# A two-layer encoder step on one core: low parts of the paired weights on VectorE, later transposes of v, and separate PSUM banks for the heads' outputs

## The chip, the cores and the metric

The kernel is one program on one core of a Trainium2 chip. The time is the device time of an execution in microseconds (us); the number compared is the median of the runs. TensorE (PE) does the matrix products, VectorE (DVE) and ScalarE (ACT) the element-wise work and the copies out of PSUM, GpSimd (POOL) a little element-wise work and the issue of some DMAs, and SyncE (SP) issues most DMAs.

## What is computed

One inference step of an encoder with two layers over 512 prompt frames and 64 frames of a running stream, 576 columns in all, with a model width of 2048. Layer 0 is gated linear attention, layer 1 a convolution module. Cut to what matters here, layer 0 is:

```python
proj = h @ w_in                       # h: rmsnorm of x; w_in: 2048 x 6160
q, k, v, r, a1 = jnp.split(proj, ...) # 1024, 1024, 2048, 2048, 16 columns
loga = jax.nn.log_sigmoid(a1 @ w_a2 + b_a) / GATE_NORM
# per head (4 heads, dk 256, dv 512), in chunks, with a decaying state S:
b = jnp.cumsum(ac, axis=-2)
att = jnp.where(mask, einsum('td,sd->ts', qc * exp(b), kc * exp(-b)), 0.0)
o = att @ vc + (qc * exp(b)) @ S
S = exp(b_last)[:, None] * S + (kc * exp(b_last - b)).T @ vc
y = (rmsnorm(o) * silu(r)) @ w_out
```

Layer 1 and the final norm follow; the change does not touch them. All tensors are float32.

## The kernel before

**Precision.** A float32 product is made of three TensorE products in a faster float format: a weight is split into a high part (whi, a rounded copy on ACT) and a low part (wlo, raw minus whi), the activations likewise (names that end in h and l), and hi x hi, hi x lo and lo x hi are added. A unit is a pair (whi, wlo) of 128 x 8 x 128 elements; each of the two has four buffers, used in turn. `to_unit` makes a unit. Its low part is made in one of two ways: by a subtraction on DVE (L126), or, when `src` is given, by a negated copy on ACT (L128) to which a DMA issued by POOL adds the weights from DRAM once more (L129).

**The pair stage** (126 to 498 us of the profile). Fourteen pairs of 128-column weight blocks (eight pairs of v, the two of head 1's q and k, four of r) are each computed by `run_full` in a Strassen-like scheme: seven products of 24 matmuls in place of eight (`step(0)` to `step(6)`, with sums S1 to S4 of activation blocks and differences of weight blocks on DVE, L184). The four raw weight blocks of a pair are r1 (two buffers, ra and rb), r2 and r4 (two buffers shared), and r3 (one buffer). A step makes sure that the units up to four steps ahead have been asked for (`ensure`, LEAD = 4). The results are collected in PSUM tiles d11, d12, d21 (a pool of four banks) and db, and copied to two SBUF tiles ta and tb (`t1`, `t2`) of a tag s2 with six buffers. `done` then handles each of the two. For q, k and r it writes the tile to DRAM. For v (`v_done`) it transposes the tile on TensorE into token order (`to_tok`: four transposes into ptv, one into puv, in PSUM tiles of the tag ms), splits it on ACT and DVE and writes four pieces to the DRAM tensor vd with SP's queue.

**The heads** (498 to 792 us). For each of four heads: the decay (`decay`: small matmuls pz at L778, then exponentials, logarithms and scans on ACT and DVE), the scores (`attention`: pa at L844 and L854, transposes of the keys), the outputs (`output`: po at L889 for the prompt, pq at L894 and L897 for the stream, copied by ACT at L891 and by DVE at L898), the states (`states`: pS at L920) and the norm (m_o at L458). The remaining projections (`tile`, 24 products of 48 matmuls, tiles ps) are interleaved by the scheduler with the head's own work. The PSUM tiles pz, pa, pt, pu, po, pq, pS and m_o all share the two banks of the tag ms. The projections take two banks each from `main_tile`: two of three times from the pool of four banks, every third time from the two banks of the tag main.

**What sets the order.** The program is written in the order of the Python code; a list scheduler then orders each engine's instructions by priority and readiness at build time. Weight splitting has a raised priority. On the chip each engine runs its list in that order and waits on semaphores.

Of the kernel before, what the change touches and what calls it, by code (L numbers as in the profile page):

```python
# [11 lines left out]
F32 = mybir.dt.float32  # L12
# [5 lines left out]
P = 128  # L18
# [31 lines left out]
def emit(nc, tc, x, wg, wa1, wa2, wgo, wc, wco, par, s0, y, sp_out, ss_out, cv_out):  # L50
# [30 lines left out]
    def psum_pool(key, name, bufs):  # L81
        psum[key] = tc.tile_pool(name=name, bufs=bufs, space=PSUM)
        return psum[key].__enter__()
# [6 lines left out]
    px = psum_pool("e", "pse", 1)  # L90
    pool_s = [px]
# [12 lines left out]
    def tmp(name, w=T, dt=F32):  # L104
        return s2.tile([P, w], dt, tag="s2", name=name)
# [8 lines left out]
    def load_raw(src, half, name, p=None, tag="raw"):  # L114
        raw = (p or wraw).tile([P, 8, P], F32, tag=tag, name=name)
        state["dma"] = nc.sync.dma_start(raw, src[:, half * 8 : half * 8 + 8, :])
        return raw

    def to_unit(i, raw, w=8, src=None):

        hi = whl.tile([P, 8, P], F32R, tag="whi", name=f"whi{i}")
        lo = whl.tile([P, 8, P], F32R, tag="wlo", name=f"wlo{i}")
        with tc.high_priority(offset=PRIO):
            nc.scalar.activation(hi[:, :w, :], raw, AF.Copy)  # L124
            if src is None:
                nc.vector.tensor_tensor(lo[:, :w, :], raw, hi[:, :w, :].bitcast(F32), ALU.subtract)  # L126
            else:
                nc.scalar.activation(lo, raw, AF.Copy, scale=-1.0)  # L128
                nc.gpsimd.dma_start(lo, src, accum_op=ALU.add)  # L129
        ready[i] = (hi, lo)  # L130
# [46 lines left out]
    def plan_full(w1, w2, ra):  # L177


        d = {}  # L180

        def diff(out, a, b):
            with tc.high_priority(offset=PRIO):
                nc.vector.tensor_tensor(out, a, b, ALU.subtract)  # L184

        def u0(i):
            d["r1"] = load_raw(w1, 0, f"raw{i}", sp, ra)
            to_unit(i, d["r1"], src=w1[:, :8, :])

        def u1(i):  # L190
            d["r2"] = load_raw(w2, 0, f"raw{i}")
            diff(d["r1"], d["r2"], d["r1"])
            to_unit(i, d["r1"])

        def u2(i):
            d["r3"] = load_raw(w2, 1, f"raw{i}", sp, "r3")
            diff(d["r2"], d["r3"], d["r2"])
            diff(d["r1"], d["r3"], d["r1"])
            to_unit(i, d["r1"])

        def u4(i):
            d["r4"] = load_raw(w1, 1, f"raw{i}")
            to_unit(i, d["r4"], src=w1[:, 8:, :])

        def u5(i):
            diff(d["r1"], d["r4"], d["r1"])
            to_unit(i, d["r1"])

        chunks.extend([u0, u1, u2, lambda i: to_unit(i, d["r2"]), u4, u5,
                       lambda i: to_unit(i, d["r3"], src=w2[:, 8:, :])])  # L210

    def ensure(n):
        while state["n"] < min(n, len(chunks), state["cap"]):
            i = state["n"]
            state["n"] += 1
            chunks[i](i)
# [27 lines left out]
    rot = {"n": 0}  # L244

    def bank(name):
        return psb.tile([P, 512], F32, tag="bank", name=name)[:, :HT]

    def main_tile(name):

        rot["n"] += 1
        if pool_s[0] is not None and rot["n"] % 3 == 0:
            return [pool_s[0].tile([P, 512], F32, tag="main", bufs=2, name=f"{name}_{j}")[:, :HT] for j in range(2)]
        return [bank(f"{name}_{j}") for j in range(2)]

# [123 lines left out]
    def operand(n, k):  # L379
        if n in sums8:  # L380
            return [sums8[n][k // 2][:, part, k % 2, :] for part in range(2)]
        j = 0 if n in ("A11", "A12") else 1
        k += 8 if n in ("A12", "A22") else 0
        return [a[k][:, j * HT : (j + 1) * HT] for a in (ah, al)]

    def prod8(dst, n, unit, first):
        hi, lo = unit
        for k in range(8):
            a, b = operand(n, k)
            for i, (w, v) in enumerate(((hi, a), (hi, b), (lo, a))):  # L390
                nc.tensor.matmul(dst, w[:, k, :], v, start=first and k == 0 and i == 0,  # L391
                                 stop=k == 7 and i == 2, skip_group_check=True)

    def run_full(c, f1, f2, func, done, middle=None):

        c11, c12, c21 = (bank(f"d{n}_{f1}") for n in ("11", "12", "21"))
        pb = pool_s[0].tile([P, 512], F32, tag="main", bufs=2, name=f"db_{f1}")[:, :HT]
        sh = tmp(f"sh{f1}", HT)
        t1, t2 = tmp(f"ta{f1}"), tmp(f"tb{f1}")
        w = t2[:, HT:]  # L400

        def step(i, dst, n, first):
            ensure(c + i + LEAD)
            prod8(dst, n, ready.pop(c + i), first)

        add = nc.vector.tensor_tensor
        step(0, c11, "A11", True)
        nc.scalar.activation(sh, c11, AF.Copy)
        step(1, c12, "S1", True)
        if middle:  # L410
            middle()
        step(2, pb, "S2", True)
        add(sh, sh, pb, ALU.add)
        step(3, c21, "S3", True)
        add(w, sh, c21, ALU.add)
        add(w, w, c12, ALU.add)
        step(4, c11, "A12", False)
        nc.scalar.activation(t1[:, :HT], c11, func)
        step(5, c21, "A22", False)
        add(t1[:, HT:], sh, c21, ALU.add)  # L420
        if func != AF.Copy:
            nc.scalar.activation(t1[:, HT:], t1[:, HT:], func)
        done(f1, t1)
        step(6, c12, "S4", False)
        add(t2[:, :HT], sh, c12, ALU.add)
        if func != AF.Copy:
            nc.scalar.activation(t2, t2, func)
        done(f2, t2)

    def run_plain(c, f1, f2, addend, evac):  # L430

# [113 lines left out]
    def page(i, shape, name, dt=F32):  # L545

        return sp.tile(shape, dt, tag=i if isinstance(i, str) else f"pg{i}", name=name)
# [33 lines left out]
    for half, aw in enumerate(a1w):  # L581
        src = a1r[:, 8 * half : 8 * half + 8, :].unsqueeze(2).broadcast_to([P, 8, 3, RANK])
# [61 lines left out]
    w2 = page(9, [96, 1024], "w2s", F32R)  # L644
# [105 lines left out]
    for i, (b, n) in enumerate(gla_pairs):  # L750
        run_full(base_p + 7 * i, b, b + 1, AF.Silu if n == "r" else AF.Copy, v_done if n == "v" else to_dram,
                 restore if i == len(gla_pairs) - 1 else None)
    sums8.clear()
    pools.pop().__exit__(None, None, None)

# [120 lines left out]
    def output(h):  # L876
        d = hd[h]
        q, att, v = d["qs"], d["att"], d["v"]
        d["s0"] = s0t = gp.tile([P, 2, DVH], F32, tag="s0", name=f"s0_{h}")
        nc.sync.dma_start(s0t, s0[:, 2 * h : 2 * h + 2, :])  # L880
        ob = big.tile([P, 4, T], F32, tag="big", name=f"o{h}")
        sq = stat.tile([P, T], F32, tag="ssq", name=f"osq{h}")
        pairs = products(v, att)
        for vt in range(4):
            vc = slice(vt * P, vt * P + P)
            po = px.tile([P, 512], F32, tag="ms", bufs=2, name=f"po{h}{vt}")
            for i in range(4):
                for n, (a, b) in enumerate(pairs):
                    nc.tensor.matmul(po[:, i * P : TP], a[:, i, vc], b[:, OFFS[i] : OFFS[i] + TP - i * P],  # L889
                                     start=(i == 0 and n == 0), stop=(i == 3 and n == 2), skip_group_check=True)  # L890
            nc.scalar.activation(ob[:, vt, :TP], po, AF.Copy)  # L891
            po = px.tile([P, 512], F32, tag="ms", bufs=2, name=f"pq{h}{vt}")
            for dt in range(2):
                nc.tensor.matmul(po[:, :TS], s0t[:, dt, vt * P : (vt + 1) * P], q[:, dt, :],  # L894
                                 start=(dt == 0), stop=False)
            for n, (a, b) in enumerate(pairs):
                nc.tensor.matmul(po[:, :TS], a[:TS, 4, vc], b[:TS, 1280:1344], start=False, stop=(n == 2))  # L897
            nc.vector.tensor_copy(ob[:, vt, TP:T], po[:, :TS])  # L898
            add_sq(sq, ob[:, vt, :], vt == 0, f"o{h}{vt}")
        d.update(o=ob, sq=sq)  # L900
# [41 lines left out]
    def start_head(h):  # L942
        hd[h] = {}
        decay(h)
# [12 lines left out]
    def gates(h):  # L957
        for vt in range(4 if h < 3 else 1):
            rblk(h, vt)
# [10 lines left out]
    def tile(i, ins=None):  # L970
        with tc.issue_after(ins) if ins is not None else nullcontext():
            run_groups(gla_last[i : i + 1], heads_evac, base_l + 2 * i)

    start_head(0)
    scores(0)
    tile(0)
    values(0)
    for h in range(H):
# [13 lines left out]
        if h < 3:  # L992
            tile(2 * h + 3, turned)
            values(h + 1)
    gates(3)
    tile(9, turned)


# [340 lines left out]
```

## Time and profile before

| | |
|---|---|
| median of 3 runs | 1823.49 us (1821.79 to 1824.61) |
| profiled execution | 1826.77 us, span 1825.0 us |
| mean granted TensorE clock | 0.985 |
| PE busy | 1736.3 us, 95% |
| DVE, ACT, POOL busy | 59%, 52%, 29% |
| DMA, accumulating and others from POOL's queue (q0) | 99.86 MB, 27.9% of 16 engines' span |
| DMA from SP's queue (q1) | 202.33 MB, 36.8% |

A row of the stages gives the length of a stretch, then for PE, weight loads (PEld), DVE, ACT and POOL the busy time and the number of instructions in it, then the granted clock, the mean busy share of the 16 DMA engines and GB/s. A row of waits says which engine and line waited for which, the sum in us, how many times, and the longest. A row of groups ends with busy time, mean ns of one, and idle time before it with what ended it. A row of the chain or the timeline starts with the time from the start of the span and a length. Names stand without buffer numbers there.

### The profile page before, as it was taken

The page shows a single profiled execution, that of the slowest core. Times are in us where ns is not written, and L with a number is a line of the kernel's source. Part 1 is how long each engine was busy: PE and PEld are TensorE (multiplying, and loading weights), DVE is VectorE, ACT ScalarE, POOL GpSimd, SP SyncE. Part 2 cuts the span into 40 slices and gives each one's busy share as a digit, 9 for nine tenths or more (in the row PEclk, how much of TensorE's full clock was granted, in tenths as well). Part 3 has the DMA queues.
Part 4 walks back from the last instruction along what each step waited for, and adds up shares of the span by engine and source line. Part 5 has one row for each costly group of instructions (what it writes and reads, how often), then busy time and mean ns, then how long its engine had stood idle before and what let it go on. Part 6 is the DMA issues. An engine that isn't in the chain of part 4 may idle for free.

```text
span 1825.0 us, 31131 instructions
## 1 busy us (share of the span) xinstructions
PE 1736.3 (95%) x12606; PEld 1702.0 (93%) x12606; DVE 1069.2 (59%) x1580; ACT 943.9 (52%) x1271; POOL 526.1 (29%) x497
## 2 busy tenths in 40 slices
PE   9999988899898998999999999999999999999996
PEld 8998888889898887999999999999999999999995
DVE  7764453544334355195557788878888761185554
ACT  7754443435565556463236555656555574453333
POOL 3100100001121333202222455545555452223221
PEclk9999999999999999999999999999999999999998
DMA  7966857667796776544444777777777768713323
GB/s 241 242 157 165 206 134 190 173 168 181 189 271 173 211 225 185 146 165 153 144 133 140 166 165 165 165 165 166 163 166 165 178 144 185 158 54 133 110 94 129
DMA packets 114944, 304.18 MB, mean 167 GB/s; under 512 B 11344, under 2 KB 37840, under 8 KB 113776
## 3 DMA queue, kind: packets, MB, share of 16 engines
q1 hardware_dynamic: 87632, 202.33, 36.8%
q0 software_dynamic: 27168, 99.86, 27.9%
q8 instruction: 99, 1.62, 0.4%
q14 instruction: 45, 0.37, 0.1%
HBM read 264.70 MB, written 37.45 MB: 166 GB/s over the span
## 4 chain that ended last, share of the span: by engine, by line
PE 74%; DMA 10%; DVE 7%; issue 5%; ACT 3%; SPq 1%; POOL 0%; DVEq 0%; ACTq 0%; POOLq 0%
PE ps L227 15%; PE ps L230 15%; PE ps L224 15%; PE c L337 8%; PE c L328 6%; PE d L391 5%; DMA raw<-wg 4%; DMA wlo<-wg 3%; PE db L391 2%; PE pS L920 1%; PE cb L328 1%; DVE c L1174 1%; PE po L889 1%; DVE wlo L126 1%; PE pq L337 1%
## 5 line engine op out<-in xcount | busy, mean ns | idle before, releaser
L124 ACT ACTIVATE whi<-raw 128x1024 fp32r<-128x1024 f32 x296 | 312.5, 1058 | 515.9 <-PE ps L227 170.0
L227 PE MATMUL ps<-h1l,whi 128*128 128x288 f32 x1536 | 329.7, 296 | 0.0
L224 PE MATMUL ps<-h1h,whi 128*128 128x288 f32 x1536 | 329.7, 296 | 0.0
L230 PE MATMUL ps<-h1h,wlo 128*128 128x288 f32 x1536 | 329.5, 296 | 0.0
L1111 DVE SCALAR_TENSOR_TENSOR acc<-ux,pr,acc 128x606 f32<-128x606 f32 x352 | 297.7, 852 | 11.8 <-ACT acc L1101 2.2
L230 PEld LDWEIGHTS ps<-h1h,wlo 128*128 128x128 f32 x1536 | 248.3, 189 | 0.0
L227 PEld LDWEIGHTS ps<-h1l,whi 128*128 128x128 f32 x1536 | 248.3, 189 | 0.0
L224 PEld LDWEIGHTS ps<-h1h,whi 128*128 128x128 f32 x1536 | 248.2, 189 | 0.0
L126 DVE TENSOR_TENSOR wlo<-raw,whi 128x1024 fp32r<-128x1024 f32 x126 | 157.1, 1247 | 113.9 <-ACT whi L124 112.5
L129 POOL DMA_DIRECT2D wlo<-wg x78 | 67.9, 871 | 506.0 <-ACT wlo L128 350.0
L128 ACT ACTIVATE wlo<-raw 128x1024 fp32r<-128x1024 f32 x170 | 177.2, 1042 | 0.0
L1109 POOL TENSOR_TENSOR sd<-sd,sd 128x606 f32<-128x606 f32 x96 | 153.3, 1597 | 72.5 <-ACT sd L1105 71.2
L391 PE MATMUL d<-nh,wlo 128*128 128x288 f32 x448 | 135.8, 303 | 13.5 <-DMA wlo<-wg 13.5
L608 POOL TENSOR_TENSOR ssq<-ssq,sq_x 128x576 f32<-128x576 f32 x35 | 63.3, 1810 | 295.6 <-ACT sq_x L607 289.4
L129 POOL DMA_DIRECT2D wlo<-wc x92 | 80.8, 879 | 218.7 <-ACT wlo L128 165.3
L391 PE MATMUL d<-nh,whi 128*128 128x288 f32 x448 | 135.5, 303 | 0.0
L391 PE MATMUL d<-nl,whi 128*128 128x288 f32 x448 | 135.0, 301 | 0.0
L184 DVE TENSOR_TENSOR raw<-raw,raw 128x1024 f32<-128x1024 f32 x56 | 68.4, 1223 | 86.4 <-DMA raw<-wg 73.4
L1105 ACT ACTIVATE sd<-ux,pr 128x606 f32<-128x606 f32 x112 | 87.3, 793 | 55.8 <-POOL sd L1109 55.8
L227 PE MATMUL ps<-nl,whi 128*128 128x288 f32 x480 | 108.7, 303 | 0.0
L230 PE MATMUL ps<-nh,wlo 128*128 128x288 f32 x480 | 105.2, 300 | 2.8 <-DMA wlo<-wg 2.8
L224 PE MATMUL ps<-nh,whi 128*128 128x288 f32 x480 | 106.8, 304 | 0.0
(542 smaller groups left out, 3904.4 us busy)
## 6 DMA issues: line engine op xcount, KB each, us to landing
raw<-wc SPq DMA_DIRECT2D x96, 512.0 KB, 4.9
raw<-wg SPq DMA_DIRECT2D x94, 512.0 KB, 6.0
wlo<-wc POOLq DMA_DIRECT2D x92, 512.0 KB, 7.6
wlo<-wg POOLq DMA_DIRECT2D x78, 512.0 KB, 8.5
raw<-wco SPq DMA_DIRECT2D x26, 512.0 KB, 3.8
raw<-wgo SPq DMA_DIRECT2D x25, 512.0 KB, 4.3
ld<-pd SPq DMA_DIRECT2D x29, 288.0 KB, 6.9
vd<-v SPq DMA_DIRECT2D x32, 256.0 KB, 6.5
```

The source lines that it names most:

```text
L124: nc.scalar.activation(hi[:, :w, :], raw, AF.Copy)
L126: nc.vector.tensor_tensor(lo[:, :w, :], raw, hi[:, :w, :].bitcast(F32), ALU.subtract)
L128: nc.scalar.activation(lo, raw, AF.Copy, scale=-1.0)
L129: nc.gpsimd.dma_start(lo, src, accum_op=ALU.add)
L224: nc.tensor.matmul(ps[j], hi[:, kk, :], ah[k][:, j * HT : (j + 1) * HT], start=st, stop=False)
L227: nc.tensor.matmul(ps[j], hi[:, kk, :], al[k][:, j * HT : (j + 1) * HT], start=False, stop=False)
L230: nc.tensor.matmul(ps[j], lo[:, kk, :], ah[k][:, j * HT : (j + 1) * HT], start=False, stop=sp)
L328: nc.tensor.matmul(dst, w[:, o + k, :], v, start=start and k == 0 and i == 0, stop=stop and k == 3 and i == 2, skip_group_check=True)
L337: nc.tensor.matmul(dst[j], w[:, k, :], v[:, j * HT : (j + 1) * HT], start=start[j] and k == 0 and i == 0, stop=stop[j] and k == 7 and i == ...
L391: nc.tensor.matmul(dst, w[:, k, :], v, start=first and k == 0 and i == 0, stop=k == 7 and i == 2, skip_group_check=True)
L1109: nc.gpsimd.tensor_tensor(side, side, t, ALU.add)
L1111: nc.vector.scalar_tensor_tensor(a, v3(u[:, w : w + CW]), cw(w), a, ALU.mult, ALU.add)
```

## The change

Three edits:

1. In the pair stage all low parts are made on DVE: three units of each pair lose `src`.
2. The calls of `done` are kept in a list `later`, and the first two steps of the next pair each call one of them after their product; what is left runs after the last pair.
3. In the heads po takes its tiles from the tag main in place of ms, and the projections' tiles always come from the pool of four banks while the flag `heads` is set.

```diff
@@ plan_full
-            to_unit(i, d["r1"], src=w1[:, :8, :])
+            to_unit(i, d["r1"])
...
-            to_unit(i, d["r4"], src=w1[:, 8:, :])
+            to_unit(i, d["r4"])
...
-                       lambda i: to_unit(i, d["r3"], src=w2[:, 8:, :])])
+                       lambda i: to_unit(i, d["r3"])])
@@ main_tile
-        if pool_s[0] is not None and rot["n"] % 3 == 0:
+        if pool_s[0] is not None and rot["n"] % 3 == 0 and not rot.get("heads"):
@@ run_full
+    later = []
...
             prod8(dst, n, ready.pop(c + i), first)
+            if i < 2 and later:
+                later.pop(0)()
...
-        done(f1, t1)
         step(6, c12, "S4", False)
...
-        done(f2, t2)
+        later.extend([lambda: done(f1, t1), lambda: done(f2, t2)])
@@ after the loop over gla_pairs
+    while later:
+        later.pop(0)()
@@ output
-            po = px.tile([P, 512], F32, tag="ms", bufs=2, name=f"po{h}{vt}")
+            po = px.tile([P, 512], F32, tag="main", bufs=2, name=f"po{h}{vt}")
@@ before and after the heads
+    rot["heads"] = True
     start_head(0)
...
     gates(3)
+    rot.update(n=0, heads=False)
     tile(9, turned)
```

TensorE at the end of the first v pair, before: the last matmuls of the sixth product (d21), two transposes of ta, then the seventh product (d12).

```order
L391 MATMUL d21_4_1459<-nh14_1031,wlo21_1526 128x288
L391 MATMUL d21_4_1459<-nh15_1036,whi21_1525 128x288
L391 MATMUL d21_4_1459<-nl15_1037,whi21_1525 128x288
L391 MATMUL d21_4_1459<-nh15_1036,wlo21_1526 128x288
L729 MATMUL ptv4_1652<-ident_89,ta4_1462 128x128 x2
L391 MATMUL d12_4_1458<-S4_0_1050,whi22_1554 128x288 x2
```

And after: ta's transposes stand behind the first product of the second pair (d11_6) and ahead of its second (d12_6).

```order
L391 MATMUL d11_6_1678<-nh7_996,whi23_1584 128x288
L391 MATMUL d11_6_1678<-nl7_997,whi23_1584 128x288
L391 MATMUL d11_6_1678<-nh7_996,wlo23_1585 128x288
L732 MATMUL ptv4_1716<-ident_89,ta4_1461 128x128 x4
L735 MATMUL puv4_1723<-ident_89,ta4_1461 64x128
L391 MATMUL d12_6_1679<-nh0_957,whi24_1616 128x288
```

The first transposes have moved two products and are in one piece; those of tb (behind 22 matmuls of the next pair's second product before) now stand behind 15 matmuls of its third.

DVE around the change from the first to the second v pair, before (raw23 to raw25 are the second pair's r1, r2 and r3; sh, tb and ta collect results):

```order
L126 TENSOR_TENSOR wlo21_1526<-raw16_1263,whi21_1525 128x1024
L413 TENSOR_TENSOR sh4_1461<-sh4_1461,db_4_1460 128x288
L415 TENSOR_TENSOR tb4_1463<-sh4_1461,d21_4_1459 128x288
L416 TENSOR_TENSOR tb4_1463<-tb4_1463,d12_4_1458 128x288
L184 TENSOR_TENSOR raw23_1585<-raw24_1617,raw23_1585 128x1024
L184 TENSOR_TENSOR raw24_1617<-raw25_1667,raw24_1617 128x1024
L126 TENSOR_TENSOR wlo24_1621<-raw23_1585,whi24_1620 128x1024
L184 TENSOR_TENSOR raw23_1585<-raw25_1667,raw23_1585 128x1024
L420 TENSOR_TENSOR ta4_1462<-sh4_1461,d21_4_1459 128x288
```

After:

```order
L126 TENSOR_TENSOR wlo21_1524<-raw16_1263,whi21_1523 128x1024
L417 TENSOR_TENSOR sh4_1460<-sh4_1460,db_4_1459 128x288
L126 TENSOR_TENSOR wlo22_1553<-raw18_1380,whi22_1552 128x1024
L419 TENSOR_TENSOR tb4_1462<-sh4_1460,d21_4_1458 128x288
L420 TENSOR_TENSOR tb4_1462<-tb4_1462,d12_4_1457 128x288
L126 TENSOR_TENSOR wlo23_1585<-raw23_1582,whi23_1584 128x1024
L184 TENSOR_TENSOR raw23_1582<-raw24_1613,raw23_1582 128x1024
L184 TENSOR_TENSOR raw24_1613<-raw25_1645,raw24_1613 128x1024
L126 TENSOR_TENSOR wlo24_1617<-raw23_1582,whi24_1616 128x1024
L424 TENSOR_TENSOR ta4_1461<-sh4_1460,d21_4_1458 128x288
```

The low parts of units 22 and 23 are new in DVE's list, and ta stands ahead of the second difference with r3, still behind the first.

ACT in the second head, in the decay of the third (c2_2: absolute value, exponential, logarithm; o1 are copies of po, p33 copies of a projection, whi129 and wlo129 parts of a weight unit), before:

```order
L782 ACTIVATE c2_2_5926<-eq2_5927 128x1152
L783 ACT_TABLE_LOAD
L783 ACTIVATE c2_2_5926<-c2_2_5926 128x1152
L891 ACTIVATE o1_6092<-po10_6094 128x512
L124 ACTIVATE whi129_6556<-raw129_6554 128x1024
L967 ACT_TABLE_LOAD
L967 ACTIVATE p33_0_6381<-ps124_0_0_6269 128x288
L128 ACTIVATE wlo129_6557<-raw129_6554 128x1024
L967 ACTIVATE p33_1_6384<-ps124_0_1_6270 128x288
L784 ACT_TABLE_LOAD
L784 ACTIVATE c2_2_5926<-c2_2_5926 128x1152
```

After:

```order
L896 ACTIVATE o1_6050<-po12_6098 128x512
L896 ACTIVATE o1_6050<-po13_6122 128x512
L787 ACTIVATE c2_2_5884<-eq2_5885 128x1152
L788 ACT_TABLE_LOAD
L788 ACTIVATE c2_2_5884<-c2_2_5884 128x1152
L789 ACT_TABLE_LOAD
L789 ACTIVATE c2_2_5884<-c2_2_5884 128x1152
```

All four po copies now stand ahead of the absolute value, and the copies p33 and the weight unit behind the logarithm. On TensorE the same move shows between the last decay matmul of this head and the next head's first scores: before, 9 projection matmuls, the four groups po and pq and the pS stand there; after, 78 projection matmuls, the four pq and the pS, and the po stand ahead.

## The prediction

> **What bounds the kernel now.** I read the page's busy shares first, then the stages, then what TensorE waits for in the two stages that the change touches.
>
> ```profile
> PE 1736.3 (95%) x12606; PEld 1702.0 (93%) x12606; DVE 1069.2 (59%) x1580; ACT 943.9 (52%) x1271; POOL 526.1 (29%) x497
> 126.00:498.00 372.00, 336.00 (x2435) 329.35 (x2435) 172.22 (x215) 169.13 (x218) 38.24 (x45) 0.98 0.69 174
> 498.00:792.00 294.00, 271.97 (x1782) 249.78 (x1781) 117.62 (x263) 172.74 (x268) 77.52 (x108) 0.97 0.75 210
> ...
> PE d L391 <- DMA wlo<-wg: 20.0, 19, 2.5
> PE ptv L729 <- DVE ta L420: 15.9, 7, 4.3
> ```
>
> TensorE is the bound as a whole. The two stage rows (length, then PE, weight load, DVE, ACT, POOL busy, then granted clock) leave it 36.0 us idle of 372 in the pair stage and 22.0 of 294 in the heads, with DVE under half busy in both. Two waits make all of the pair stage's idle time: 20.0 for low parts that a DMA finishes, 15.9 for a transpose whose input DVE has not written.
>
> How far the pair stage is from what its matmuls need comes from these rows of the tile d, the transposes and the chain that ended last:
>
> ```profile
> L391 PE MATMUL d<-nh,whi x448: 290/295/589, 126.4 to 494.1; 128*128 128x288 f32 x150
> ...
> L391 PE MATMUL d<-S,wlo x224: 290/295/610, 136.2 to 498.1; 128*128 128x288 f32 x112
> ...
> L732 PEld LDWEIGHTS puv<-ident,ta x8: 109/111/177, 151.0 to 349.7; 128*64 128x64 f32 x8
> ...
> 184.52 0.44 PE ptv L729 x4
> 184.96 0.11 PE puv L732
> ...
> 185.34 3.21 PE db L391 x24
> ...
> 188.64 0.47 DVE sh L413
> ...
> 190.00 1.02 SPq L116
> ...
> 191.11 10.06 DMA raw<-wg
> ...
> 202.41 1.23 DVE wlo L126
> ...
> 203.66 1.23 DVE raw L184
> 204.89 0.38 DVE ta L420
> ...
> 211.98 3.21 PE db L391 x24
> ```
>
> A product of 24 matmuls takes 3.2 us, so a pair (7 products) takes 22.4, and a v pair 1.1 more for its ten transposes. The stage needs 14 x 22.4 + 8 x 1.1 = 322.4 us; it takes 498.1 - 126.4 = 371.7. So 49.3 us are lost: 36.0 idle, 0.02 x 372 = 7.4 to the clock, and the remaining 6 are the pipeline's refill at the 26 waits. The v pairs lose most: (349.7 - 151.0) / 7 = 28.4 a pair against 23.5. The chain shows their loop: the raw block r3 (one buffer) is loaded for 10.06 us, DVE stands behind it in order (difference, low part, difference), only then writes ta, and TensorE stands at the transposes of ta.
>
> **The change, part by part.**
>
> ```profile
> L126 DVE TENSOR_TENSOR wlo<-raw,whi 128x1024 fp32r<-128x1024 f32 x54 | 66.0, 1222 | 38.8 <-ACT whi L124 38.8
> L184 DVE TENSOR_TENSOR raw<-raw,raw 128x1024 f32<-128x1024 f32 x52 | 63.6, 1223 | 85.2 <-DMA raw<-wg 72.2 <-ACT wlo L128 9.6 <-DMA vd<-v 2.9
> L723 DVE TENSOR_TENSOR v<-ptv,v 128x512 fp32r<-128x512 f32 x16 | 11.0, 687 | 17.5 <-ACT v L722 17.5
> L413 DVE TENSOR_TENSOR sh<-sh,db 128x288 f32<-128x288 f32 x14 | 6.3, 454 | 10.3 <-PE db L391 10.3
> ...
> L124 ACT ACTIVATE whi<-raw 128x1024 fp32r<-128x1024 f32 x98 | 102.8, 1056 | 159.1 <-DVE raw L184 86.8 <-PE d L391 24.6 <-issue 20.6
> L128 ACT ACTIVATE wlo<-raw 128x1024 fp32r<-128x1024 f32 x44 | 45.8, 1041 | 0.0
> ...
> L129 POOL DMA_DIRECT2D wlo<-wg x44 | 38.1, 865 | 350.6 <-ACT wlo L128 256.5 <-ACT sh L408 93.0 <-ACT ta L418 1.1
> ...
> DMA to landing us min/median/max: 5.6/8.9/17.3
> ...
> raw<-wg SPq DMA_DIRECT2D x32, 512.0 KB, 8.0
> ```
>
> *Low parts.* 3 x 14 = 42 units lose the negated copy on ACT (1.04 us) and the accumulating DMA (8.9 us to landing), and gain a DVE subtraction (1.22 us). The ring of whi/wlo has four places and a product takes 3.2 us, so a unit may be filled only in the 9.6 us before its turn. Now 1.06 + 1.04 + 8.9 = 11.0 us: too late by about a microsecond, three times a pair, which is the 20.0. Afterwards 1.06 + 1.22 = 2.3 us, with 7 us to spare for queueing: all 20.0 go. ACT gets 44 us lighter; DVE 42 x 1.22 = 51 heavier. Per v pair DVE then has 7 x 1.22 + 4 x 1.22 + 4 x 0.45 + 2 x 0.69 plus two small ones, about 17.4 us in 23.5: room, if its order does not hold it up. What it stands behind is the difference with r3. That loop is now: load L, difference 1.22, one low part and ta (1.7), difference 1.22, high part 1.06, low part 1.22, product 3.2, the next unit's high and low part that free r3 (1.06 + 1.7), issue 0.4, so L + 12.8. It reaches 23.5 when L is 10.7. The median of raw loads is 8.0 in this part of the stage, and the 42 half-megabyte accumulations that shared the engines with them are gone. I take the loop as no longer deciding. SP's order: r3's load is still behind the four writes of the second v block, as before, whose data come some 2 us before r3 is free by the durations above.
>
> *Transposes.* ta's go from between the sixth and the seventh product (and into the next pair) to behind the next pair's first product, tb's into its third. Each stands at least 3.2 us behind what it reads, so the 15.9 goes; nothing is added on TensorE. Who waits later: ACT's and DVE's copies of v, the writes to vd, and ta and tb stay longer in the six s2 buffers. With sh of the next pair and four v tiles that is seven names; the transposes free ta before the second block's tiles are wanted, so I cost it at nothing. A late vd write (6.5 us to land) would delay only ta of the next pair, four products later.
>
> Together: 49.3 less 4 us for a first pair that starts as before and a few late r3: **45 us**. Bounds: 49 if nothing is left; 20.0 + 15.9 - 13 = 23 if r3's loop costs 1.6 us in each of 8 v pairs (L of 12.3).
>
> *Heads.* What TensorE waits for between 498 and 792, and one passage from the decay matmuls (L778) of a head to its scores (L844):
>
> ```profile
> PE pq L894 <- ACT o L891: 5.0, 3, 2.0
> ...
> PE ps L230 <- DMA wlo<-wg: 2.8, 1, 2.8
> PE pq L894 <- DVE o L898: 2.7, 2, 1.3
> PE po L889 <- ACT o L891: 1.6, 2, 0.8
> ...
> PE pS L920 <- DVE s L923: 1.4, 1, 1.4
> ...
> 622.45 0.30 PE L778 MATMUL pz<-a,w 96*128 96x288 f32 x1
> ...
> 627.52 0.50 PE L889 MATMUL po<-athi,vhi 128*128 128x512 f32 x1 [0.82 <-ACT o L891]
> ...
> 629.49 0.61 PE L894 MATMUL pq<-qsm,s 128*128 128x64 f32 x4
> ...
> 653.22 0.71 PE L844 MATMUL pa<-eq,c 128*128 128x128 f32 x4 [0.95 <-DVE v_o L481]
> ...
> 626.89 0.58 ACT L891 ACTIVATE o<-po 128x512 f32<-128x512 f32 x1
> ...
> 631.40 1.28 ACT L784 ACT_TABLE_LOAD   x1
> ```
>
> The passage takes 30.8 us, most of it a chain through ACT and DVE. In the new order the four po of a head run ahead of the decay matmuls and 69 more of the 0.133 us projection matmuls (3.2 / 24) behind them. That puts 69 x 0.133 - 4 x 1.97 = 1.3 us more TensorE work in the passage. The chain gets shorter: between its exponential and the table load for its logarithm ACT now does 626.89 to 631.40 of other work (a po copy, two p copies, a weight unit), all of it elsewhere in the new order: 30.8 - 4.5 = 26.3. So a passage gains 4.5 + 1.3 = 5.8, three of them 17; the first low part of the stage, 2.8 late, gains perhaps 2; the clock (0.03 x 294 = 8.8 lost) gives back 4. New: pS takes the banks of pq, whose copies by DVE stand behind the scan, about 1 us in three heads. Sum **20 us** of 30.8 lost (22.0 + 8.8). The 10.7 us that pq, po and pS wait for banks are inside the passages, so they are not added; if the chain keeps its length, they only move to pa. Bounds: 3 x 1.3 + 2 = 6, and 30. That main tiles now have two pairs of banks costs nothing: one fills for 12.8 us while ACT copies the other in 0.8.
>
> After 792 the instructions on TensorE stand as before. Profiled execution: 1826.8 (span 1825.0 and 1.8 around it) - 45 - 20 = 1761.8. It lies 3.3 above the median of the runs, so **1759 us**.
>
> One of those terms is the clock. It falls after short waits:
>
> ```profile
> 248.00:252.00 4.00, 2.08 (x16) 1.84 (x15) 1.50 (x3) 2.23 (x3) 1.20 (x2) 1.00 1.03 253
> 252.00:256.00 4.00, 4.00 (x21) 4.00 (x20) 0.64 (x1) 0.00 (x0) 0.54 (x1) 0.57 1.00 248
> ```
>
> TensorE idles 1.9 us of the first four, and the next four run at 0.57. I take these dips as caused by the waits, so they go with them. The Trainium skill ("TensorE: Matmul & The Clock Gate", on the HAM clock gate) says that the clock halves after at least one idle window of about 3.4 us. By that rule the DMA waits, of at most 2.5 us, would not cool it, the 7.4 us would stay, and the sum would be 1766; the row shows a dip after a shorter idle time, so I go by the row.
>
> **Rivals.**
> 1. *r3's loop stays the bound of the v pairs*: L stays near 12 (it was 10.06 in the chain), 25 us a v pair instead of 23.5: 13 us more, 1772. For it: 72.2 us of DVE's idle time is for raw. Against: less traffic.
> 2. *The heads' chain keeps its length*: TensorE's work is the same in sum, and the bank waits turn into a wait of pa: 6 instead of 20, 1773. For it: pa already waits for DVE in the last row of the passage. Against: ACT's 4.5 us of other work leave the chain by the order.
> 3. *The dips of the clock are not the waits'*: 7 us stay, 1766.
> 4. *Slower: DVE becomes the bound of the pair stage.* DVE serves in order and now idles 199.8 us of 372 there, nearly all behind something (85.2 at L184, 38.8 at L126). If those waits are its place in the loop and do not shrink, the 51 us come on top: 1759 + 45 + 51 = 1855. It decides from 28.4 - 17.4 = 11 us of unavoidable waiting per v pair. Against: most of it is for raw and for PE, which both come earlier. The Trainium skill ("Perfetto Trace Analysis", on optimizing Scalar/DVE operations) would rather move work off a saturated DVE to ACT; here the DVE row says 46%.
>
> **How the numbers follow.** Forecast 0.55, rival 1 0.15, rival 2 0.13, rival 3 0.06, rival 4 0.05, and 0.06 for more than the forecast (both floors, 1745). Low 1745: 49 and 30. High 1790: rivals 1 and 2 together (1786) and a little. 0.2% (3.6 us) is about what runs of this kernel can tell from no change. Faster 0.94, same 0.01, slower 0.05.
>
> **What would show it.** Right: no wait of L391 for a DMA of wlo; none of the transposes for ta; puv at 23.5 to 24.5 us a pair; pair stage about 327 us with its clock at 1.00; raw loads nearer 6 us; heads about 274 us with pq's waits gone and short ones at pS and m_o. Wrong: TensorE waiting for wlo from DVE L126 (rival 4 if long, rival 1 if DVE then waits for raw), or po waiting for its masked scores or for v.

## The result, and the profile after

The changed kernel takes 1776.91 us (median of 4 runs, 1772.69 to 1777.91), the kernel before 1824.05 us beside it: ratio 0.9736, 95% interval 0.9715 to 0.9758. That is 47 us less. The forecast was 1759 with a range of 1745 to 1790: the side was right, the gain was put 18 us too high. Of the two terms of the sum, one came out above its upper bound and the other not at all. One execution of one experiment further down (o in halves, with the norm's sums and pS in the banks of main) ran at a granted clock of 0.842 and took 1861.87 us; it is left out of that experiment's numbers.

The stages of the changed kernel, cut at the last product of the pair stage and the last projection of the heads (length; PE, weight load, DVE, ACT and POOL busy; clock; DMA share; GB/s):

```profile
125.45:446.90 321.45, 321.45 (x2438) 321.45 (x2436) 221.10 (x256) 136.14 (x179) 3.71 (x5) 1.00 0.45 136
446.90:740.80 293.90, 273.31 (x1777) 251.30 (x1776) 133.85 (x277) 173.96 (x272) 75.50 (x107) 0.96 0.74 208
```

The kernel before, cut at the same instructions:

```profile
126.36:498.40 372.04, 336.04 (x2436) 329.39 (x2435) 172.22 (x215) 169.47 (x219) 38.24 (x45) 0.98 0.69 174
498.40:792.00 293.60, 271.57 (x1779) 249.38 (x1778) 117.62 (x263) 172.34 (x268) 77.52 (x108) 0.97 0.75 210
```

The pair stage lost 50.6 us: TensorE has no idle time in it and its clock is at 1.00. The heads lost nothing (293.6 and 293.9). What is before and after them is the same within a microsecond.

In the pair stage the transposes come every (315.1 - 151.2) / 7 = 23.4 us, the v pair's own need:

```profile
L735 PEld LDWEIGHTS puv<-ident,ta x8: 111/111/111, 151.2 to 315.1; 128*64 128x64 f32 x8
...
L184 DVE TENSOR_TENSOR raw<-raw,raw 128x1024 f32<-128x1024 f32 x52 | 63.5, 1222 | 4.3 <-DMA raw<-wg 3.5
```

The second row is the weight differences on DVE in the stage, now idle 3.5 us for raw blocks instead of 72.2. Raw loads and the writes of v, from issue to landing (last column, median us), over the whole pair stage, before:

```profile
raw<-wg SPq DMA_DIRECT2D x55, 512.0 KB, 7.4
wlo<-wg POOLq DMA_DIRECT2D x43, 512.0 KB, 8.9
vd<-v SPq DMA_DIRECT2D x32, 256.0 KB, 6.5
```

and after:

```profile
raw<-wg SPq DMA_DIRECT2D x56, 512.0 KB, 4.3
vd<-v SPq DMA_DIRECT2D x32, 256.0 KB, 4.6
```

In the heads the waits of TensorE moved:

```profile
PE pa L849 <- DVE v_o L484: 6.0, 3, 4.2
PE po L894 <- ACT o L896: 4.2, 3, 1.8
PE ps L230 <- DMA wlo<-wg: 2.5, 2, 1.3
PE pS L925 <- ACT so L933: 1.8, 2, 1.2
```

```profile
ACT o L896 <- PE po L894: 13.4, 8, 3.2
...
ACT o L896 <- DMA spill<-o: 10.1, 3, 4.5
```

The waits of pq are gone. Those of po have grown from 1.6 to 4.2 us, and what they wait for is a copy on ACT that waits for something new (second fence, ACT's waits in the heads): the storing (spill) of the previous head's o, 10.1 us in three waits. Those of pa for v_o have grown too; before they were these:

```profile
PE pa L844 <- DVE v_o L481: 2.9, 3, 1.0
```

One of the waits for the spill (ACT ahead of the decay of the fourth head; then the chain that ended last at that place) is the longest:

```profile
623.29 1.09 ACT L896 ACTIVATE o<-po 128x512 f32<-128x512 f32 x2 [4.48 <-DMA spill<-o]
```

```profile
617.29 5.77 DMA spill<-o
...
623.29 0.61 ACT o L896
...
623.94 3.64 PE po L894 x20
```

The three passages from a head's last decay matmul pz to the next head's first score pa (length, PE busy, clock, DMA share, GB/s), before:

```profile
557.80:590.20 32.40, 27.63 (x161) 1.00 0.62 161
622.50:653.20 30.70, 24.39 (x121) 0.94 0.52 136
683.90:714.70 30.80, 24.44 (x122) 0.94 0.53 139
```

and after:

```profile
503.90:534.00 30.10, 25.97 (x162) 1.00 0.57 161
565.90:593.10 27.20, 23.88 (x143) 0.99 0.47 127
627.70:655.20 27.50, 23.62 (x140) 0.97 0.47 130
```

They did get shorter, by 2.3, 3.5 and 3.3: 9.1 us together. The rest of the heads grew by 9.4, from 293.6 - 93.9 = 199.7 to 293.9 - 84.8 = 209.1. TensorE's idle time there went from 22.0 - 17.4 = 4.6 to 20.6 - 11.3 = 9.3 us, and the time lost to the clock outside the passages from 5.1 to 10.8.

### The profile page after: what moved, and what is told of

It is laid out like the page before. It is cut to its first block, busy times and chain, and to the rows that moved or that the text cites. A ratio compares the mean times of both kernels' runs of the same rounds, so it can differ in the third digit from the quotient of the medians.

```text
span 1774.5 us, 31017 instructions
## 1 busy us (share of the span) xinstructions
PE 1722.7 (97%) x12606; PEld 1695.9 (96%) x12606; DVE 1126.0 (63%) x1622; ACT 906.9 (51%) x1229; POOL 491.8 (28%) x455
## 4 chain that ended last, share of the span: by engine, by line
PE 81%; DVE 6%; DMA 6%; ACT 3%; issue 2%; POOL 1%; SPq 0%; ACTq 0%; DVEq 0%; POOLq 0%
PE ps L230 14%; PE ps L224 14%; PE ps L227 14%; PE d L391 14%; PE c L337 9%; PE c L328 6%; PE db L391 2%; DMA wlo<-wg 2%; PE po L894 1%; DMA spill<-o 1%; PE cb L328 1%; DVE c L1181 1%; PE pS L925 1%; PE pq L337 1%; PE pq L444 1%
## 5 line engine op out<-in xcount | busy, mean ns | idle before, releaser
L126 DVE TENSOR_TENSOR wlo<-raw,whi 128x1024 fp32r<-128x1024 f32 x168 | 208.4, 1241 | 132.3 <-ACT whi L124 130.1
L1116 POOL TENSOR_TENSOR sd<-sd,sd 128x606 f32<-128x606 f32 x96 | 153.5, 1599 | 73.4 <-ACT sd L1112 72.2
L129 POOL DMA_DIRECT2D wlo<-wg x36 | 31.8, 882 | 478.7 <-DVE tb L420 335.7
L128 ACT ACTIVATE wlo<-raw 128x1024 fp32r<-128x1024 f32 x128 | 133.6, 1044 | 0.1
L391 PE MATMUL d<-nh,wlo 128*128 128x288 f32 x448 | 131.9, 294 | 0.0
L391 PE MATMUL d<-S,whi 128*128 128x288 f32 x448 | 90.3, 295 | 0.0
```

Source lines behind the costliest of these rows:

```text
L1116: nc.gpsimd.tensor_tensor(side, side, t, ALU.add)
```

## Experiments

The numbers of each run stand against runs of the kernel before on the same chip. Several chips were used, on which the kernel before took 1819.3 to 1821.8 us in the median (1824.05 in the result above); so the difference of two runs by their times and by their ratios can disagree by about 3 us. For short, the three edits are called by their numbers in the section on the change.

**Edit 1 alone.** Only the three `src` arguments are dropped.

```diff
-            to_unit(i, d["r1"], src=w1[:, :8, :])
+            to_unit(i, d["r1"])
...
-            to_unit(i, d["r4"], src=w1[:, 8:, :])
+            to_unit(i, d["r4"])
...
-                       lambda i: to_unit(i, d["r3"], src=w2[:, 8:, :])])
+                       lambda i: to_unit(i, d["r3"])])
```

> Edit 1 alone (all low parts of the pair stage on DVE; transposes and heads as before). Separate theory: the 20.0 us of waits for accumulated low parts go, with about half of the five dips of the clock (4 us), the 15.9 us at the transposes stay: 1823 - 24 = 1799. Shared-loop theory: in the v pairs both waits are ends of one loop through r3, so the 10.5 us of low-part waits that lie in v pairs reappear at the transposes of ta and only the 9.6 us behind the v pairs and two dips (3.4) are gained: about 1810, with ptv waiting 20 us or more. DVE-bound theory: slower than 1823.

Measured: 1777.46 us (1771.8 to 1779.32), ratio 0.9766 (0.9742 to 0.979). Its pair stage and raw loads:

```profile
124.53:446.03 321.50, 321.50 (x2438) 321.50 (x2436) 222.36 (x257) 135.95 (x179) 3.70 (x5) 1.00 0.44 136
```

```profile
raw<-wg SPq DMA_DIRECT2D x56, 512.0 KB, 4.1
```

All three theories missed. Edit 1 takes the whole pair-stage gain, the 15.9 us of waits for ta included, although the transposes stand where they stood, right behind their product. So these waits were a consequence of the accumulating DMAs too.

**Edit 2 alone.** `run_full` keeps `later`, as in the change; low parts by DMA and heads as before.

```diff
             prod8(dst, n, ready.pop(c + i), first)
+            if i < 2 and later:
+                later.pop(0)()
...
-        done(f1, t1)
...
-        done(f2, t2)
+        later.extend([lambda: done(f1, t1), lambda: done(f2, t2)])
```

> Edit 2 alone (transposes of v behind the next pair's first products; low parts by DMA and heads as before). Separate theory: the 15.9 us at ptv go and about half of the dips (4 us): 1823 - 20 = 1803, the 20 us for wlo stay. Shared-loop theory: TensorE then arrives earlier at the next unit and waits for wlo there instead: the wait for wlo grows from 20 to some 30 us and the time is about 1815.

Measured: 1833.81 us (1829.74 to 1836.4), ratio 1.0075 (1.0048 to 1.0101): slower, so both theories missed. Its pair stage takes 384.7 us. The two waits of DVE for DMAs between 126 and 350 us, for raw blocks and for the writes of v, and these writes:

```profile
DVE raw L184 <- DMA raw<-wg: 49.6, 8, 9.1
DVE tb L419 <- DMA vd<-v: 37.3, 6, 10.1
```

```profile
vd<-v SPq DMA_DIRECT2D x32, 256.0 KB, 10.5
```

On DVE the next pair's tb waits for a buffer of s2 whose v tile is still being written to vd, 37.3 us in six waits; tb had no such wait before. Later transposes mean later v tiles and later writes, and the writes take 10.5 us in place of 6.5. The transposes still wait for ta (18.2 us in the whole stage). TensorE waits for that tb in turn, 8.5 us in five waits, and still 17.3 us for low parts. That the buffers are the cause is read from the trace; no run with a seventh buffer was made.

**Edits 1 and 2 without edit 3.**

```diff
-            po = px.tile([P, 512], F32, tag="main", bufs=2, name=f"po{h}{vt}")
+            po = px.tile([P, 512], F32, tag="ms", bufs=2, name=f"po{h}{vt}")
...
-        if pool_s[0] is not None and rot["n"] % 3 == 0 and not rot.get("heads"):
+        if pool_s[0] is not None and rot["n"] % 3 == 0:
```

> Edits 1 and 2 without edit 3 (heads as before). If the heads' edit is worth nothing in the changed kernel, as the two traces read (293.6 and 293.9 us): same as the changed kernel, 1773 to 1778, heads 293 to 295. If edit 3 gained its 20 us and the new pair stage cost the heads as much (another state of the queues at their start), this comes out near 1797 with heads of some 314 us.

Measured: 1775.55 us (1774.5 to 1777.01), ratio 0.9762 (0.9745 to 0.9779); its heads take 293.2 us. The same as the changed kernel.

**Edit 3 alone**, the reverse of this diff on the kernel before:

> Edit 3 alone (po in the banks of main, projections always in the pool of four; pair stage as before). If edit 3 is worth nothing: 1820 to 1827, heads 292 to 295 with the same new waits (pa for v_o, po for o, pS for so). If it gains by itself and lost it only behind the new pair stage: 1803 to 1810, heads about 275.

Measured: 1820.63 us (median of 10 runs, 1813.66 to 1829.79), ratio 0.9999 (0.9981 to 1.0017). Edit 3 is worth nothing with either pair stage, and the new wait is there with the old one too (ACT, in the heads):

```profile
ACT o L891 <- DMA spill<-o: 7.9, 3, 3.5
```

**Is it the traffic?** In the changed kernel, POOL's queue copies the same half megabyte per unit within DRAM, to a place nobody reads:

```diff
+    def traffic(i, src):
+        n = state["junk"] = state.get("junk", -1) + 1
+        t = sp.tile([P, 1], F32, tag="junk", bufs=4, name=f"junk{i}")
+        with tc.high_priority(offset=PRIO):
+            ins = nc.gpsimd.tensor_copy(t, ready[i][0][:, 0, :1].bitcast(F32)).ins
+            with tc.issue_after(ins):
+                nc.gpsimd.dma_start(scratch[n], src)
...
             to_unit(i, d["r1"])
+            traffic(i, w1[:, :8, :])
```

and so for r4 and r3.

> The changed kernel with the removed traffic put back without its use: for each of the 42 units whose low part moved to DVE, POOL's queue copies the same half megabyte within DRAM to a place nobody reads, issued when the unit's high part is there. The order of the other four engines is unchanged. Traffic theory (the waits for ta went because raw loads fell from 7.4 to 4.3 us): raw loads are back at 7 us or more, the loop through r3 reaches 23.4 us in some v pairs, TensorE waits again and the pair stage takes 325 to 345 us: 1781 to 1800. Unit theory (they went because a unit is ready 2.3 instead of 11.0 us after its turn): the pair stage stays at 321 us without a wait: 1775 to 1779.

Measured: 1775.36 us (1774.18 to 1780.41), ratio 0.9749 (0.9722 to 0.9777); pair stage 321.5 us without a wait. But raw loads came only to 5.8 us, below the 7 that the theory asked for, so this run does not decide.

**The same on edit 1 alone, with busier DMA engines:** the copy is written in pieces of 512 bytes.

```diff
-                nc.gpsimd.dma_start(scratch[n], src)
+                nc.gpsimd.dma_start(scratch[n].rearrange("p (k two) c -> p k two c", two=2)[:, :, 0, :], src)
```

> Edit 1 alone (transposes right behind their product, where a late r3 shows at once) with traffic put back: for each of the 42 units POOL's queue copies the same half megabyte within DRAM, here written in pieces of 512 bytes so that the DMA engines are busier than with the plain copy (which brought raw loads only to 5.8 us); the order of the other four engines is that of edit 1 alone. Traffic theory: raw loads are back at 7 us or more in the stage, the loop through r3 passes 23.4 us in some v pairs, the transposes wait for ta again (10 us or more in sum) and the pair stage takes 330 to 345 us: 1786 to 1800. Unit theory: no wait for ta, pair stage 321 to 324, 1775 to 1780.

Measured: 1788.55 us (1785.38 to 1790.29), ratio 0.9818 (0.9798 to 0.9838), 11 us above edit 1 alone. Raw loads, what TensorE waits for in the pair stage, and a turn of the chain (in this kernel L743 are the transposes, L434 ta, L125 and L127 the two parts of a unit, L405 the products):

```profile
raw<-wg SPq DMA_DIRECT2D x52, 512.0 KB, 6.8
```

```profile
PE ptv L743 <- DVE ta L434: 10.4, 5, 2.9
```

```profile
202.00 1.07 ACT whi L125
203.09 1.24 DVE wlo L127
204.35 9.31 DMA raw<-wg
...
216.12 0.38 DVE ta L434
...
216.54 0.44 PE ptv L743 x2
...
224.26 3.08 PE db L405 x23
...
227.41 1.07 ACT whi L125
```

The waits for ta are back, 10.4 us of the 15.9, and the pair stage takes 334.5 us. Nothing but the traffic differs: the other four engines run in the same order. A turn with a load of 9.31 takes 227.41 - 202.00 = 25.4 us, 2 more than the v pair needs. Raw loads came to 6.8 us, just under the 7 that this run, too, was to reach, but the effect is there: with all low parts still made on DVE, traffic alone brings the waits back. So the traffic theory holds, and the unit theory, which expected no wait, does not. The copies only stand in for the accumulations, and whether the missing 5.5 us are their lighter traffic or the late units is not told apart. Read this way, the accumulations cost twice: once as late low parts, and once by making r3's load so long that its loop passed the pair's need.

**And with edit 2 under the same traffic** (all three edits, copies in pieces of 512 bytes):

> The changed kernel (all three edits) with the same traffic in pieces of 512 bytes as the run with edit 1 alone, which brought raw loads to 6.8 us there and 10.4 us of waits for ta back; the order of the other four engines is that of the changed kernel. Theory that edit 2 is a cushion (a late ta has a product of 3.2 us more to arrive, and the longest of those waits was 2.9): no wait at the transposes, pair stage 321 to 323 us, 1774 to 1779, some 12 us less than edit 1 alone under the same traffic. Theory that edit 2 is worth nothing or costs time under traffic, as by itself (v tiles and their writes to vd hold the s2 buffers longer): pair stage 332 us or more, 1786 or more.

Measured: 1777.24 us (1775.32 to 1777.68), ratio 0.9763 (0.9726 to 0.98).

```profile
124.38:445.85 321.47, 321.47 (x2438) 321.47 (x2436) 219.77 (x256) 134.55 (x178) 78.82 (x86) 1.00 0.63 202
```

No wait, and 11 us less than edit 1 alone under that traffic. So edit 2 is a cushion that the changed kernel does not need: worth nothing in a quiet stage, 11 us in a busy one, and a loss where the writes of v become the late ones. Its loads were shorter too (median 5.4, against 6.8), and how much of the 11 us comes from that and how much from the product ahead of the transposes is not told apart.

**The heads: o in two halves.** The tile o has one buffer; here its two halves have one each, so that the first copies wait for the first spills only. (The other tile of the tag, in layer 1, is halved in the same way.) In the trace every engine keeps the order of the changed kernel.

```diff
-        ob = big.tile([P, 4, T], F32, tag="big", name=f"o{h}")
+        ob = big_halves(f"o{h}")
...
+    def big_halves(name):
+        return Halves([big.tile([P, 2, T], F32, tag=f"big_{i}", name=f"{name}_{i}") for i in range(2)])
```

> The changed kernel with the tile o of a head in two halves of two rows of 128 columns each with a buffer of its own, so that the first two copies of po wait only for the first two spills of the previous head. Theory that the earlier po brought a wait for the spill onto ACT, ahead of the decay's exponentials: the 4.2 us of po's waits fall to 2 or less and the passages get about 1.5 us shorter each, one dip less: 1777 - 6 = 1771. Theory that the copies of po are not in the chain: same, 1774 to 1779.

Measured: 1766.36 us (1764.7 to 1768.66), ratio 0.9695 (0.9671 to 0.972): about 10 us below the changed kernel, against 6 expected.

```profile
445.45:729.85 284.40, 268.13 (x1777) 247.75 (x1776) 134.41 (x278) 173.60 (x272) 75.51 (x107) 0.98 0.76 215
```

The heads take 284.4 us. ACT's copies of po no longer wait for a spill (10.1 us before the halves), po waits for nothing, the passages are as long as in the changed kernel (84.9 us in sum) and the rest is back at 284.4 - 84.9 = 199.5. This is where edit 3's gain was. By the ratios the gain is 7.5 us in place of 10. It is no chance of one trace: with a single buffer for o the same heads take 293.9, 294.3 and 293.6 us, in the changed kernel and in the two runs that add traffic to it. Of the 9.5 us, 4.3 are idle time of TensorE, about what po had waited, and about 5 are the clock, with four slow windows (see the last section) in place of seven. That split is soft, since the three traces have seven, eight and five.

**The halves without edit 3** (edits 1 and 2 and the halves):

> Edits 1 and 2 with the heads as before (without edit 3), and o in two halves. Theory that edit 3 made the wait for the spill by moving po ahead of the decay's exponentials: without edit 3 nobody waits for the spill, so the halves change nothing: 1773 to 1778. Theory that the halves help whatever the order (another cause than that wait): 1764 to 1769.

Measured: 1773.87 us (1770.96 to 1776.11), ratio 0.9733 (0.9714 to 0.9752): not clearly faster than edits 1 and 2, and its heads take 295.1 us. ACT's copies of po wait for no spill here, nor did they without the halves. The wait that the halves take away is made by edit 3; neither alone shortens the heads, and both together gain 9 us by the times and 12 by the ratios.

**The norm's sums in the banks of main.**

```diff
-                m = pool_s[0].tile([P, 512], F32, tag="ms", bufs=2, name=f"m_{name}{j}")
+                m = pool_s[0].tile([P, 512], F32, tag="main" if rot.get("heads") else "ms", bufs=2,
+                                   name=f"m_{name}{j}")
```

> The changed kernel with the norm's sums m_o of the heads in the banks of main instead of ms, so that the next head's scores pa no longer wait for v_o. Theory that the heads' time now hangs on who shares the two banks of ms: the 6 us of pa's waits and the dips of the clock behind them (534, 592, 654 us: up to 8 us) go: 1777 - 10 = 1767. Theory that the chain of the decay on ACT and DVE sets the passages whatever the banks: pa waits for its own inputs (eq, c) instead and nothing changes: 1774 to 1779.

Measured: 1769.45 us (1766.42 to 1770.34), ratio 0.9707 (0.9677 to 0.9737): 7 us below the changed kernel, 10 expected. The waits of pa for v_o are gone, so the banks of ms did bind there. ACT's waits for the spill doubled, and this version is faster all the same:

```profile
ACT o L896 <- DMA spill<-o: 20.9, 3, 7.6
```

So that wait is not lost time as such. What TensorE has of it is the wait of po for the copies, 4.6 us here and 4.2 in the changed kernel; why 20.9 us on ACT cost no more than 10.1 was not followed up.

**Both together:**

> The changed kernel with o in two halves and m_o in the banks of main (pS stays in ms). If the two waits are separate places: the gains of each alone (10.5 and 7.4 us) add to about 16, 1761, idle time in the heads 12 us or less. If they are ends of one chain (the decay behind po's copies on ACT): no better than o in two halves alone, 1764 to 1768.

Measured: 1770.62 us (1767.47 to 1774.19), ratio 0.9717 (0.9695 to 0.9738). No sum, and not better than the halves alone: TensorE now waits at the states, and ACT's copies of po wait for a spill again, 8.3 us in two waits.

```profile
PE pS L938 <- DVE s L941: 6.6, 2, 3.4
PE pS L938 <- DVE o L916: 3.6, 2, 1.9
```

**And pS in the banks of main too:**

> The changed kernel with o in two halves, and m_o and pS both in the banks of main, so that ms is left to pz, pa, the transposes and pq. If the heads' waits are those for banks and for the spill: 20.6 us of idle time and 12 of clock fall by more than half, heads 278 us, 1777 - 16 = 1761. If the chain of the decay sets the passages: 1772 to 1779.

Measured: three runs from 1768.23 to 1773.2, ratio 0.972 (0.9689 to 0.9751). The 1761 of the first theory was missed. Why the gains of the halves and of m_o do not add is open: the halves leave every engine's order as it was, but moving m_o changes the scheduler's order in the heads, and no run separates that from the banks. The lowest median is that of the change with o in two halves, 1766.4 us.

## Why the prediction was right, and where not

*Low parts, 20.0 us.* Right: no wait for wlo is left in the pair stage.

*Transposes, 15.9 us.* The waits went, but the step that gave them to edit 2 failed. Edit 1 alone removes them, because r3 arrives in time, and edit 2 alone adds time. The sentence that the accumulations are gone was in the working, as an argument against rival 1; it should have been a gain of edit 1, with the same 15.9 not counted as edit 2's own. The sum came out near because edits that remove the same wait were counted once. That the number came out for these 15.9 us is luck.

*Who waits later, "I cost it at nothing".* Failed for edit 2 by itself: the late vd write held up tb, not ta, by 37.3 us on DVE. With edit 1 beside it, in the changed kernel, the writes land in 4.6 us and DVE waits for writes of v for 4.8 us in all, and TensorE for nothing.

*The pair term, 45 with bounds 23 and 49.* 50.6, above the upper bound. The 4 us kept back for a first pair and late r3 were not lost, and the floor was put at 322.4 where the stage takes 321.5.

*The loop through r3, L + 12.8 with its limit at 10.7.* Too short a loop for transposes behind their product: under traffic a turn took 25.4 at a load of 9.31, which is L + 16.1 and a limit of 7.3. The chain of that turn shows why: from the transposes of ta to the end of the product for whose buffers the next high part waits it stays on TensorE for 227.34 - 216.54 = 10.8 us, where the prediction had one product of 3.2. The stage before, with a median of 7.4, was past such a limit, if it held there; its units were made in another way, and no run changed its loads. With the loads at 4.3 the error did not matter.

*The clock.* Five dips in the pair stage, 8.5 us, went with the waits, so rival 3 is out there. The windows of 3.41 us ahead of the five had 1.85 to 3.12 us of idle time, none of them a whole window. The Trainium skill ("TensorE: Matmul & The Clock Gate", on the HAM clock gate), which has the clock halve after at least one idle window of about 3.4 us, differs from this measurement, and the measurement decides.

*Heads, 20 us.* Measured -0.3. Each passage was to gain 4.5 + 1.3: they gained 3.0 in the mean, and TensorE's work in them did not grow. The step that failed is the one that looked only at banks. Po and its copy run ahead of the decay's exponentials, so the copy into o comes while the previous head's o is still being stored from the same single buffer. That wait stands on ACT, in front of the exponentials and the logarithm, and was on no list. Nor was the longer wait of pa for v_o, 2.9 us before and 6.0 after, which the move of m_o takes away. The 2 us for a late low part at the start of the heads were not gained (waits of ps for wlo: 2.8 us before, 2.5 after), nor the 4 us from the clock: 11.9 us of dips in this trace, 8.5 before. Rival 2 came nearest, with 6 us for the heads and 1773, but by the wrong mechanism: the chain did get shorter, and the gain was spent outside it. That its sum fell within 4 us of the measured time is luck too, since it put the gain of the pair stage 5.6 us too low and that of the heads 6.3 too high.

*Rival 4, DVE as the bound.* Out: DVE is busy 221 of 321 us, its idle time at L184 fell from 85.2 to 4.3.

In the profiled execution: 1825.0 - 50.6 (pair stage) + 0.3 (heads) with the start 0.9 shorter and the rest 0.7 longer makes 1774.5, which is its span. Against the forecast of 1761.8 for it, it took 1776.2. The other 3.5 us of the 18 come from the last step: the forecast took off 3.3, by which the profiled execution before lay above its median, and the one after lies 0.7 below its own.

## What to carry to other kernels

The DMAs that did arithmetic on the way saved an engine's instruction here but cost in two places, their own 8.9 us to landing and the time of the loads beside them, 7.4 us in place of 4.3. Ask of each other wait in the stage whether it would go with the traffic before giving it an edit of its own. When instructions are moved forward, follow every buffer that they write, in SBUF as well as in PSUM, to its last reader: the wait comes with them, and on an engine that runs in order it stands in front of everything behind. An edit that measures as nothing may be a gain and a loss of equal size; the shorter passages showed the gain, and a second small edit freed it.

## What the runs showed of the hardware

The clock's dips come in steps. Cut at the right places, the rows read 0.50 or 1.00 (PE busy, clock, DMA share, GB/s), before:

```profile
248.82:252.23 3.41, 1.49 (x11) 1.00 1.00 249
252.23:255.65 3.42, 3.42 (x16) 0.50 1.04 252
```

```profile
631.09:634.50 3.41, 1.90 (x12) 1.00 0.77 189
634.50:637.92 3.42, 2.86 (x17) 1.00 1.00 227
637.92:641.33 3.41, 1.94 (x13) 1.00 0.89 312
641.33:644.74 3.41, 3.41 (x10) 0.50 0.02 6
```

and in the changed kernel:

```profile
650.34:653.75 3.41, 2.02 (x9) 1.00 0.44 125
653.75:657.17 3.42, 2.58 (x10) 0.50 1.00 250
657.17:660.58 3.41, 3.41 (x14) 0.50 1.06 329
...
687.89:691.30 3.41, 3.41 (x12) 0.50 0.15 29
691.30:694.72 3.42, 3.42 (x14) 0.50 0.00 0
```

Each dip in these traces lasts one, two or three windows of 3.41 us on a fixed grid and costs 1.7 us a window (three only in kernels without edit 3). How a dip starts goes by the window ahead: in the two stages, before and after, each window at full clock with 1.8 us or more idle is followed by a slow one (first row: 1.9 idle); of the other runs, the one with all three edits and traffic in small pieces has one with as much that is not. From 1.39 to 1.76 us of idle time it goes either way (1.90 busy is followed by full speed, 1.94 and 2.02 by half), and with less than that no dip starts in these two traces, though in that of edit 3 alone one starts after 0.9. So the sum of idle time is not the whole rule; matmuls in the windows differ, and that was not tried. How long a dip lasts does not go by it either: the last two rows show a slow window without any idle time, and the next one is slow as well. So several short waits in one window can cost as much as a long one, and the same waits spread over more windows may cost none: in these two traces the heads after have 1.4 us less idle time than before (20.6 against 22.0) and 3.4 us more of dips, seven windows against five.
